# Seven block products instead of eight in the second product of an MLP, on one core

## The chip, the cores and the metric

One core of a Trainium2 chip runs one program for the whole layer. The metric is the time of one execution in microseconds (us) on the device; lower is better. Engines are named as in the profile: PE (TensorE, matrix products), PEld (its weight loads), DVE (VectorE), ACT (ScalarE), POOL (GpSimd), SP (the engine that issues most DMAs). SBUF is the memory that all of them read, PSUM the banks that PE writes.

## The reference

One residual layer over a sequence of 2048 frames of width 1024: a normalisation, forgetting attention with 16 heads, a gated residual, a second normalisation and an MLP with a squared ReLU, all in float32. The change concerns the last product of the last line:

```python
h = rms_norm(x, norm_mlp[i]) * (1 + sc_f) + sh_f
x = x + g_f * (jnp.square(jax.nn.relu(h @ w_mlp_in[i])) @ w_mlp_out[i])
```

Here `h` is 2048 x 1024, `w_mlp_in` 1024 x 4096, `w_mlp_out` 4096 x 1024; `g_f` is one row of 1024 that scales the result.

## The kernel before

The program has stages that follow each other on all engines: projections and attention, the output projection, the MLP's first product, and the MLP's second product, the last stage and the only one that the change touches. A tile framework records the operations in the order in which the code calls them, then orders them on each engine by its own estimate of when each can start, and puts in the waits; so the order on an engine is not quite that of the code.

Float32 products are made from three products of a shorter format. `split` (L749 to L751) writes an operand as two tiles: ACT rounds it to the high part (L750), and DVE subtracts that from the operand to get the low part (L751); both inputs of the subtraction lie in SBUF. `mm3` (L135 to L139) then issues high x high, high x low and low x high into one PSUM bank. A bank holds 128 rows by 512 columns.

The MLP's first product already takes seven block products for each 2x2x2 arrangement of blocks: sums of input blocks are made on POOL (`stage`, L952), split like any operand, multiplied, and the seven results are combined by DVE on the way out of PSUM (`partial`, L987, and `finish`, L980), after which ACT takes the ReLU, POOL the square (L982), and the result `a` goes to DRAM, one tile of 128 features by 512 frames at a time (`a_d`).

The second product, before the change, is plain. The sequence has two halves of 1024 frames (`s`), each of 8 row blocks of 128 frames. The 4096 features are taken in 8 chunks (`ch`) of 4 feature blocks (`CB`). For a chunk, `chunk_ops` loads four blocks of `w2` (128x1024) and eight tiles of `a` (128x512), and splits them; it is a generator that is advanced by one operand between the products of the chunk before. For each row block and each half of the columns, 4 x 3 matmuls sum four feature blocks in one bank (`py`). DVE copies the bank to `ya` in the first chunk (L1110) and adds it in the others (L1118). In the last chunk POOL first multiplies `ya` by the gate and adds the residual `x1`, both 128x1024 (L1101, L1102), and DVE then multiplies the bank by the gate (L1113), adds it (L1114), and the row block is stored.

Of the kernel before, what the change touches and what calls it, by code (L numbers as in the profile page):

```python
# [60 lines left out]
def fox_layer(ctx, tc, x, c, norm_mix, norm_mlp, w_ada, b_ada, w_mlp_in, w_mlp_out,  # L61
              fox_w_in, fox_b_f, fox_q_norm, fox_k_norm, fox_w_out, out):
    nc = tc.nc
    x = x[0]
# [983 lines left out]
    def ring(tag, shape, dt, nm):  # L1050
# [4 lines left out]
    ny = [0]

    def y_bank(nm):
        ny[0] += 1
        if ny[0] % 3 < 2:
            return psS.tile([P, TJ], F32, tag="S", name=nm)  # L1060
        return psT.tile([P, TJ], F32, tag="T", name=nm)

    def chunk_ops(s, ch, into):
        fbs = range(ch * CB, (ch + 1) * CB)
        for t in range(2):
            for fb in fbs:
                if t == 0:
                    wr = ring("wr", [P, D], F32, f"w2r{s}_{fb}")
                    nc.sync.dma_start(wr, w2[fb * P:(fb + 1) * P, :])
                    w = ring("w", [P, 2, D], F32R, f"w2_{s}_{fb}")  # L1070
                    split(w, wr)
                    into["w"].append(w)
                    yield
                ar = ring("ar", [P, TJ], F32, f"ar{s}_{fb}_{t}")
                nc.sync.dma_start(ar, a_d[2 * s + t][fb])
                a = ring("a", [P, 2, TJ], F32R, f"a{s}_{fb}_{t}")
                split(a, ar)
                into["a", t].append(a)
                yield

    steps = [(s, ch) for s in range(NS) for ch in range(NCH)]
    chunks = {st_: {"w": [], ("a", 0): [], ("a", 1): []} for st_ in steps}
    gf = None
    for _ in chunk_ops(*steps[0], chunks[steps[0]]):
        pass
    ya = {}
    for n, (s, ch) in enumerate(steps):
        ops = chunks.pop((s, ch))
        nxt_ = [chunk_ops(*steps[n + 1], chunks[steps[n + 1]])] if n + 1 < len(steps) else []
        if gf is None:  # L1090
            gf = ring("gf", [P, D], F32, "gate_bc1")
            nc.sync.dma_start(gf, gate_d[1:2, :].broadcast_to([P, D]))
        for t in range(2 * RB):
            i = s * 2 * RB + t
            if ch == 0:
                ya[i] = ring("ya", [P, D], F32, f"ya{i}")
            y = ya[i]
            if ch == NCH - 1:
                x1 = ring("x1", [P, D], F32, f"m_x1_{i}")
                nc.sync.dma_start(x1, x1_d[i])  # L1100
                nc.gpsimd.tensor_tensor(y, y, gf, op=ALU.mult)  # L1101
                nc.gpsimd.tensor_tensor(y, y, x1, op=ALU.add)  # L1102
            for hf, cs in enumerate(halves):
                py = y_bank(f"my{n}_{t}_{hf}")
                for b in range(CB):
                    a = ops["a", t // RB][b]
                    mm3(py, (a[:, 0, blk[t % RB]], a[:, 1, blk[t % RB]]),
                        (ops["w"][b][:, 0, cs], ops["w"][b][:, 1, cs]), b == 0, b == CB - 1)
                if ch == 0:
                    nc.vector.tensor_copy(y[:, cs], py)  # L1110
                elif ch == NCH - 1:
                    yg = ring("s", [P, TJ], F32, f"yg{i}_{hf}")
                    nc.vector.tensor_tensor(yg, py, gf[:, cs], op=ALU.mult)  # L1113
                    nc.vector.tensor_tensor(y[:, cs], yg, y[:, cs], op=ALU.add)  # L1114
                    if i >= NT - RB:
                        nc.sync.dma_start(out[i * P:(i + 1) * P, cs], y[:, cs])
                else:
                    nc.vector.tensor_tensor(y[:, cs], py, y[:, cs], op=ALU.add)  # L1118
                if (t, hf) != (RB - 1, 0) and (t, hf) != (RB - 1, 1):
                    run(nxt_)  # L1120
            if ch == NCH - 1 and i < NT - RB:
                nc.gpsimd.dma_start(out[i * P:(i + 1) * P, :], y)
        while nxt_:
            run(nxt_)


# [27 lines left out]
```

## Time and profile before

| | us |
|---|---|
| median of 3 runs | 3043.84 (3041.11 to 3048.27) |
| the profiled execution | 3046.07 |
| its span, first to last instruction | 3044.4 |
| PE busy | 2760.2 (91%) |
| DVE busy | 2078.0 (68%) |
| ACT busy | 1460.2 (48%) |
| POOL busy | 1256.7 (41%) |

The shares are means over stages that differ. The last stage begins when its first operands are loaded, near 2340 us, and ends with the span. A group's row in the profile gives a line of the kernel, engine, operation, tiles written and read, shapes, count, the busy time, the mean of one, and then the idle time of the engine just before them and what ended it.

### The profile page before, as it was taken

To read this page: it belongs to the slowest core of one execution; us is meant where nothing else is said; L and a number is where in the kernel's file an instruction comes from. 1 tells how busy PE (TensorE), PEld (TensorE's weight loads), DVE (VectorE), ACT (ScalarE), POOL (GpSimd) and SP (SyncE) were. 2 spreads that over 40 slices of the span, in tenths; PEclk is the share of its full clock that TensorE was granted. 3 is DMA by queue.
4 is the path that set the end of the run, shared out by engine and by line. 5 is a ranking of instruction groups with operands and counts; after the bars stand their busy time and mean duration, and the time that the engine had idled before them with its cause. 6 is when DMAs were issued, how large, how long until landed. Compare 5 with 4: busy or idle time off the path is not lost. (4 is left out here: it accounts for less than half of the span.)

```text
span 3044.4 us, 45983 instructions
## 1 busy us (share of the span) xinstructions
PE 2760.2 (91%) x16203; PEld 2306.8 (76%) x16203; DVE 2078.0 (68%) x3659; ACT 1460.2 (48%) x2507; POOL 1256.7 (41%) x947
## 2 busy tenths in 40 slices
PE   4788888888889888897899899989998999999999
PEld 4667677777777777786687688878887888888887
DVE  6688987988888887879442765676555544664444
ACT  4466766667667766667352454443333212121210
POOL 3354554646454644544522755575542000500014
PEclk9799989999999999998999899999999999999999
DMA  8479999999999989998963666454444323442322
GB/s 278 129 172 199 217 192 215 208 210 212 215 211 204 210 173 209 180 193 185 197 231 120 186 191 191 152 158 147 139 135 151 128 95 111 138 153 97 111 91 90
DMA packets 867239, 519.22 MB, mean 171 GB/s; under 512 B 590260, under 2 KB 770556, under 8 KB 867008
## 3 DMA queue, kind: packets, MB, share of 16 engines
q1 hardware_dynamic: 862096, 498.98, 66.3%
q0 software_dynamic: 4912, 17.30, 1.6%
q8 instruction: 127, 2.08, 0.3%
q14 instruction: 104, 0.85, 0.1%
HBM read 297.92 MB, written 75.64 MB: 123 GB/s over the span
## 5 line engine op out<-in xcount | busy, mean ns | idle before, releaser
L580 DVE SCALAR_TENSOR_TENSOR ph<-L,ph 128x1024 f16<-128x1024 f32 (+7 forms) x384 | 440.2, 1157 | 81.0 <-ACT ph L568 79.1
L137 PE MATMUL my<-w,a 128*128 128x512 f32 x1024 | 396.6, 391 | 8.2 <-ACT a L750 8.1
L413 POOL TENSOR_TENSOR hl<-hl,hh 128x1024 fp32r<-128x1024 f32 x120 | 299.1, 2494 | 249.3 <-ACT hh L412 218.8
L138 PE MATMUL my<-w,a 128*128 128x512 f32 x1024 | 398.3, 390 | 0.0
L139 PE MATMUL my<-w,a 128*128 128x512 f32 x1024 | 397.4, 389 | 0.0
L568 ACT ACTIVATE ph<-L 128x1024 f16<-128x1024 f32 (+7 forms) x384 | 301.7, 804 | 174.9 <-DMA pT<-ph 150.6
L493 PE MATMUL psq<-w,hh 128*128 128x384 f32 (+1 forms) x960 | 341.2, 356 | 25.1 <-DVE v L502 12.4
L550 DVE CUSTOM_DVE_ANT_0 L<-S,F 128x1024 f32<-128x1024 f32 (+7 forms) x384 | 343.4, 905 | 24.0 <-PE S L546 9.1
L495 PE MATMUL psq<-w,hl 128*128 128x384 f32 (+1 forms) x960 | 353.0, 369 | 2.9 <-POOL hl L413 2.8
L561 ACT ACTIVATE L<-L,st 128x128 f32<-128x128 f32 (+15 forms) x256 | 306.8, 1199 | 92.5 <-DVE st L555 88.5
L494 PE MATMUL psq<-w,hh 128*128 128x384 f32 (+1 forms) x960 | 340.5, 357 | 6.0 <-POOL w L339 6.0
L606 PE MATMUL po<-v,pT 128*128 128x128 f16 x2176 | 276.5, 228 | 69.5 <-DMA pT<-ph 61.1
L543 PE MATMUL S<-kT,qT 128*128 128x512 f32 (+3 forms) x640 | 262.3, 411 | 71.0 <-DVE mx L550 62.0
L1118 DVE TENSOR_TENSOR ya<-my,ya 128x512 f32<-128x512 f32 x192 | 132.0, 689 | 235.8 <-PE my L139 235.7
L606 PEld LDWEIGHTS <-pT 128*128 128x128 f16 x2176 | 204.7, 103 | 100.2 <-DMA pT<-ph 71.9
L1101 POOL TENSOR_TENSOR ya<-ya,gate_bc 128x1024 f32<-128x1024 f32 x16 | 41.1, 2572 | 546.2 <-DVE ya L1118 546.1
L607 PE MATMUL po<-v,pT 128*128 128x64 f16 x2176 | 258.7, 200 | 0.0
L544 PE MATMUL S<-kT,qT 128*128 128x512 f32 (+3 forms) x640 | 241.1, 384 | 0.0
L137 PEld LDWEIGHTS my<-w,a 128*128 128x128 f32 x1024 | 192.8, 188 | 49.1 <-ACT a L750 8.5
L607 PEld LDWEIGHTS <-pT 128*128 128x128 f16 x2176 | 197.7, 101 | 42.6 <-issue 31.7
L750 ACT CAST w<-w2r 128x1024 fp32r<-128x1024 f32 x64 | 67.3, 1051 | 336.3 <-PE my L139 264.0
L138 PEld LDWEIGHTS my<-w,a 128*128 128x128 f32 x1024 | 193.0, 188 | 40.2
(232 smaller groups left out, 6621.4 us busy)
## 6 DMA issues: line engine op xcount, KB each, us to landing
hl<-hT_d SPq DMA_DIRECT2D x120, 512.0 KB
w_Y_A<-in_w_mlp_in_dram SPq DMA_DIRECT2D x128, 256.0 KB
a_d<-c SPq DMA_DIRECT2D x128, 256.0 KB
w2r<-in_w_mlp_out_dram SPq DMA_DIRECT2D x64, 512.0 KB
ar<-a_d SPq DMA_DIRECT2D x128, 256.0 KB
F<-nF_d SPq DMA_DIRECT2D x64, 256.0 KB
wa<-in_w_ada_dram SPq DMA_DIRECT2D x32, 512.0 KB
w_X_A<-in_w_mlp_in_dram SPq DMA_DIRECT2D x64, 256.0 KB
```

The costliest lines, as they stand in the source:

```text
L137: nc.tensor.matmul(ps, lhsT=a[0], rhs=b[0], start=first, stop=False)
L138: nc.tensor.matmul(ps, lhsT=a[0], rhs=b[1], start=False, stop=False)
L139: nc.tensor.matmul(ps, lhsT=a[1], rhs=b[0], start=False, stop=last)
L493: nc.tensor.matmul(ps[:, :n], lhsT=hh, rhs=w[:, 0, :n], start=(kb == 0), stop=False)
L494: nc.tensor.matmul(ps[:, :n], lhsT=hh, rhs=w[:, 1, :n], start=False, stop=False)
L495: nc.tensor.matmul(ps[:, :n], lhsT=hl, rhs=w[:, 0, :n], start=False, stop=(kb == KB - 1))
L550: nc.vector.tensor_tensor_reduce(out=L[:, c0:c1], in0=s2[:, :c1 - c0], in1=Fb[g, h, cch // 2][:, :c1 - c0], scale=1.0, scalar=-3.0e38, op0 ...
L561: nc.scalar.activation(L[:, :W], L[:, :W], AF.Exp, bias=st[:, h:h + 1], scale=1.0, accum_out=st[:, 2 + h:3 + h])
L568: nc.scalar.activation(ph[:, :w], L[:, s0:s0 + w], AF.Copy, scale=PSCALE)
L580: nc.vector.scalar_tensor_tensor(ph[:, w:w + c], L[:, s0:s0 + c], PSCALE, ph[:, :c], op0=ALU.mult, op1=ALU.subtract)
L606: nc.tensor.matmul(po[:, h, :], lhsT=pT[:, bb, :], rhs=v, start=(b == 0), stop=False)
L607: nc.tensor.matmul(po[:, h, 0:HD], lhsT=pT[:, nw + bb, :], rhs=v[:, 0:HD], start=False, stop=(b == nb - 1))
```

## The change

Only the last stage changes. Let the two sequence tiles of a half (512 frames each) be the index t, the two halves of the 4096 features f, and the two halves of the output columns n. Block `A{t}{f}` is a tile of `a`, block `B{f}{n}` a tile of `w2`; feature block p is paired with p + 16. Instead of the eight products A·B, seven products P1 to P7 are made of blocks and of sums of blocks: S1 = A10 + A11, S2 = S1 - A00, S3 = A00 - A10, S4 = A01 - S2, T1 = B01 - B00, T2 = B11 - T1, T3 = B11 - B01, T4 = B10 - T2. The code takes two such pairs of feature blocks at a time (`PC = 2`), so that there are 8 chunks in a half, and of these seven are done in this way. Each of the seven products is summed over the chunks in its own four tiles `E` in SBUF (7 x 4 tiles of 128x512): ACT copies the bank in the first chunk, DVE adds it in the others. In the seventh chunk the tiles are combined to the four results (`merge`, half on POOL, half on DVE). The eighth chunk is done by plain products (`last`, D0 to D3), with gate and residual as before, in tiles of 512 columns.

The sums of blocks run on POOL. Of the 28 splits of a chunk, `ON_POOL` gives the subtraction of 12 to POOL; the other 16 stay on DVE. Sums are called three products ahead of their use, splits two ahead. The split operands have a ring of 16 tiles, four products. The output is stored from SP's queue, where `x1` and all operands are loaded too.

```diff
-    RING = {"wr": 2, "ar": 4, "w": 8, "a": 12, "ya": 10, "gf": 1, "x1": 2, "s": 2}
+    RING = {"rp": 8, "op": 16, "rq": 16, "st": 8, "e": 28, "gf": 1, "x1": 2, "s": 2}
...
-    CB = 4
-    NCH = NFB // CB
+    PC = 2
+    NCH = FP // PC
...
+        def sub(self, dst, op, x, y):
+            for p in self.ps:
+                if dst in ("S1", "S2", "T1", "T2"):
+                    self.r[dst, p] = ring("st", [P, TJ], F32, f"{dst}_{self.s}_{p}")
+                    o = self.r[dst, p]
+                else:
+                    o = self.r[dst, p] = self.r[y if dst in ("S3", "T3") else x, p]
+                nc.gpsimd.tensor_tensor(o, self.r[x, p], self.r[y, p], op=op)
...
+    OPS = {"P1": ("A00", "B00"), "P2": ("A01", "B10"), "P6": ("S2", "T2"), "P7": ("S3", "T3"),
+           "P5": ("S1", "T1"), "P4": ("A11", "T4"), "P3": ("S4", "B11")}
+    ON_POOL = {"P1": 4, "P2": 4, "P5": 2, "P4": 1, "P3": 1}
+
+    def split2(raw, nm, pool):
+        w = ring("op", [P, 2, TJ], F32R, nm)
+        nc.scalar.copy(w[:, 0, :], raw)
+        (nc.gpsimd if pool else nc.vector).tensor_tensor(w[:, 1, :], raw, w[:, 0, :].bitcast(F32), op=ALU.subtract)
+        return w
...
+    def product(chunk, prod):
+        for tb in range(RB):
+            py = y_bank(f"y{prod}_{chunk.s}_{chunk.c}_{tb}")
+            gather(py, chunk.r[prod], tb)
+            if chunk.c == 0:
+                E[prod, tb] = ring("e", [P, TJ], F32, f"e{prod}_{chunk.s}_{tb}")
+                nc.scalar.copy(E[prod, tb], py)
+            else:
+                nc.vector.tensor_tensor(E[prod, tb], E[prod, tb], py, op=ALU.add)
...
+        def add(dst, src):
+            (nc.vector if tb % 2 else nc.gpsimd).tensor_tensor(E[dst, tb], E[dst, tb], E[src, tb], op=ALU.add)
...
+    PORDER = ("P1", "P2", "P6", "P7", "P5", "P4", "P3")
...
+    def base(s, t, n, tb):
+
+        i, y = (2 * s + t) * RB + tb, E[PLACE[t, n], tb]
+        x1 = ring("x1", [P, TJ], F32, f"m_x1_{i}_{n}")
+        nc.sync.dma_start(x1, x1_d[i][:, halves[n]])
+        nc.gpsimd.tensor_tensor(y, y, gf[:, halves[n]], op=ALU.mult)
+        nc.gpsimd.tensor_tensor(y, y, x1, op=ALU.add)
+
+    def last(s, t, n, ops):
+        for tb in range(RB):
+            i, y = (2 * s + t) * RB + tb, E[PLACE[t, n], tb]
+            base(s, t, n, tb)
+            py = y_bank(f"yD{s}_{t}{n}_{tb}")
+            gather(py, ops, tb)
+            yg = ring("s", [P, TJ], F32, f"yg{i}_{n}")
+            nc.vector.tensor_tensor(yg, py, gf[:, halves[n]], op=ALU.mult)
+            nc.vector.tensor_tensor(y, yg, y, op=ALU.add)
+            nc.sync.dma_start(out[i * P:(i + 1) * P, halves[n]], y)
...
+    for n, (chunk, prod) in enumerate(seq):
+        at_sums(n + 3)
+        at_splits(n + 2)
...
+        if prod[0] != "D":
+            product(chunk, prod)
+            if chunk.c == NCH - 2:
+                for tb in range(RB):
+                    merge(prod, chunk.s, tb)
```

Here `gather` is `mm3` over the pairs of a product, and `at_sums` and `at_splits` call the sums and splits of a product and the loads of the next chunk.

**The order on the engines.** DVE in the middle of a half, before: splits of `w2` and `a` between additions to `ya`.

```order
L751 TENSOR_TENSOR w2_0_24_26503<-w2r0_24_26501,w2_0_24_26503 128x1024
L751 TENSOR_TENSOR a0_24_0_26522<-ar0_24_0_26520,a0_24_0_26522 128x512
L1118 TENSOR_TENSOR ya7_25322<-my4_7_1_26473,ya7_25322 128x512
L751 TENSOR_TENSOR w2_0_25_26541<-w2r0_25_26539,w2_0_25_26541 128x1024
L751 TENSOR_TENSOR a0_25_0_26560<-ar0_25_0_26558,a0_25_0_26560 128x512
```

The same engine in the fourth chunk of the first half, with the change (`o` are split operands, `eP3` the tiles `E` of P3, `yP3` banks; the two numbers behind are half and feature block):

```order
L1114 TENSOR_TENSOR oP6S2_0_7_26209<-S2_0_7_26137,oP6S2_0_7_26209 128x512
L1137 TENSOR_TENSOR eP3_0_0_25434<-eP3_0_0_25434,yP3_0_2_0_26159 128x512
L1114 TENSOR_TENSOR oP6T2_0_7_26212<-T2_0_7_26145,oP6T2_0_7_26212 128x512
L1137 TENSOR_TENSOR eP3_0_1_25443<-eP3_0_1_25443,yP3_0_2_1_26167 128x512
L1137 TENSOR_TENSOR eP3_0_2_25452<-eP3_0_2_25452,yP3_0_2_2_26175 128x512
L1137 TENSOR_TENSOR eP3_0_3_25461<-eP3_0_3_25461,yP3_0_2_3_26183 128x512
L1114 TENSOR_TENSOR oP7S3_0_6_26263<-rA10_0_6_25883,oP7S3_0_6_26263 128x512
```

Splits of sums that POOL made (S2, T2, S3) now stand between the evictions of the products before them.

POOL before the change: the last squares of the first product are followed at once by the gate and residual of the first half's end, with nothing between.

```order
L982 TENSOR_TENSOR c10_1_15_24968<-c10_1_15_24968 128x512
L982 TENSOR_TENSOR c01_1_15_24986<-c01_1_15_24986 128x512
L1101 TENSOR_TENSOR ya0_25059<-ya0_25059,gate_bc1_25057 128x1024
L1102 TENSOR_TENSOR ya0_25059<-ya0_25059,m_x1_0_27055 128x1024
L1101 TENSOR_TENSOR ya1_25098<-ya1_25098,gate_bc1_25057 128x1024
```

POOL with the change, from the third chunk (feature blocks 4 and 5) to the fourth (6 and 7); a sum that is written over an input bears the input's name (`rA10` becomes S3):

```order
L1091 TENSOR_TENSOR S1_0_6_26131<-rA10_0_6_25883,rA11_0_6_25887 128x512
L1114 TENSOR_TENSOR oP5S1_0_4_25945<-S1_0_4_25767,oP5S1_0_4_25945 128x512
L1114 TENSOR_TENSOR oP5T1_0_4_25948<-T1_0_4_25775,oP5T1_0_4_25948 128x512
L1091 TENSOR_TENSOR S1_0_7_26133<-rA10_0_7_25885,rA11_0_7_25889 128x512
L1091 TENSOR_TENSOR S2_0_6_26135<-S1_0_6_26131,rA00_0_6_25831 128x512
L1091 TENSOR_TENSOR rA10_0_6_25883<-rA00_0_6_25831,rA10_0_6_25883 128x512
L1114 TENSOR_TENSOR oP4A11_0_4_25991<-rA11_0_4_25523,oP4A11_0_4_25991 128x512
L1091 TENSOR_TENSOR S2_0_7_26137<-S1_0_7_26133,rA00_0_7_25833 128x512
```

The next chunk's sums stand among this chunk's splits; all are 128x512 with two SBUF inputs. At the turn to the second half, POOL with the change:

```order
L1091 TENSOR_TENSOR T2_1_1_28013<-rB11_1_1_27913,T1_1_1_28009 128x512
L1091 TENSOR_TENSOR rB01_1_1_27909<-rB11_1_1_27913,rB01_1_1_27909 128x512
L1168 TENSOR_TENSOR eP3_0_1_25443<-eP3_0_1_25443,m_x1_1_1_27812 128x512
L1168 TENSOR_TENSOR eP3_0_0_25434<-eP3_0_0_25434,m_x1_0_1_27791 128x512
L1114 TENSOR_TENSOR oP2A01_1_0_28015<-rA01_1_0_27499,oP2A01_1_0_28015 128x512
L1114 TENSOR_TENSOR oP2B10_1_0_28018<-rB10_1_0_27503,oP2B10_1_0_28018 128x512
```

The residual additions for the first half's second direct product (L1168) stand between sums and splits of the second half's first chunk.

## Rows read from the trace of the kernel before

**Rows 1.** Windows: busy us (instructions) of PE, PEld, DVE, ACT, POOL; clock, DMA, GB/s.

```profile
2400.00:2590.00 190.00, 190.00 (x840) 157.34 (x839) 88.34 (x122) 37.23 (x52) 0.00 (x0) 1.00 0.29 95
2340.00:3040.60 700.60, 699.06 (x3072) 577.97 (x3072) 367.24 (x480) 137.22 (x191) 88.66 (x44) 1.00 0.36 119
```

**Rows 2.** Chain that ended last, 2300 us to the end: start us, us, what.

```profile
2335.28 3.41 DMA w2r<-in_w_mlp_out_dram
2338.71 1.05 ACT w L750
...
3039.59 0.70 DVE yg L1113
3040.32 0.69 DVE ya L1114
```

**Rows 3.** Groups of the last stage on POOL.

```profile
L1102 POOL TENSOR_TENSOR ya<-ya,m_x 128x1024 f32<-128x1024 f32 x16 | 41.4, 2590 | 1.3
L1101 POOL TENSOR_TENSOR ya<-ya,gate_bc 128x1024 f32<-128x1024 f32 x16 | 41.1, 2572 | 546.2 <-DVE ya L1118 546.1
```

**Rows 4.** Timeline of POOL, 2200 to 2209 us: start us, us, instruction, idle before.

```profile
2201.30 1.29 POOL L952 TENSOR_TENSOR S<-w_Y_A,S 128x512 f32<-128x512 f32 x1
2202.55 1.05 POOL L982 TENSOR_TENSOR c<-c 128x512 f32<-128x512 f32 x1
2205.96 1.29 POOL L952 TENSOR_TENSOR S<-w_Y_A,w_Y_A 128x512 f32<-128x512 f32 x1 [2.36 <-DMA a_d<-c]
2207.20 1.04 POOL L982 TENSOR_TENSOR c<-c 128x512 f32<-128x512 f32 x1
```

**Rows 5.** Timelines of POOL and of DVE, 2026 to 2041 us.

```profile
2032.33 1.71 POOL L952 TENSOR_TENSOR S<-w_Y_A,S 128x512 f32<-128x512 f32 x1
2034.00 1.72 POOL L952 TENSOR_TENSOR S<-w_Y_A,w_Y_A 128x512 f32<-128x512 f32 x1
2035.68 1.49 POOL L982 TENSOR_TENSOR c<-c 128x512 f32<-128x512 f32 x1
2037.13 1.28 POOL L804 TENSOR_TENSOR ht<-hr,ht 128x512 f32<-128x512 f32 x1
...
2029.72 1.52 DVE L751 TENSOR_TENSOR T<-hr,T 128x512 fp32r<-128x512 f32 x1
2031.17 1.74 DVE L751 TENSOR_TENSOR B<-hr,B 128x512 fp32r<-128x512 f32 x1
```

**Rows 6.** Groups of the quiet stretch, 2400 to 2590 us.

```profile
L1118 DVE TENSOR_TENSOR ya<-my,ya 128x512 f32<-128x512 f32 x70 | 48.3, 690 | 90.9 <-PE my L139 90.8
L751 DVE TENSOR_TENSOR a<-ar,a 128x512 fp32r<-128x512 f32 x36 | 23.6, 687 | 3.2 <-ACT a L750 3.2
L750 ACT CAST a<-ar 128x512 fp32r<-128x512 f32 x36 | 21.6, 621 | 61.7 <-PE my L139 60.8
```

**Rows 7.** Windows, 1950 to 2300 us: all; then L751, L980 (DVE), L952, L982 (POOL) alone.

```profile
1950.00:2300.00 350.00, 342.06 (x1493) 282.25 (x1492) 223.49 (x276) 144.25 (x241) 208.25 (x160) 0.99 0.45 142
...
1950.00:2300.00 350.00, 144.90 (x152) 0.99 0.45 142
...
1950.00:2300.00 350.00, 48.11 (x70) 0.99 0.45 142
...
1950.00:2300.00 350.00, 102.10 (x74) 0.99 0.45 142
...
1950.00:2300.00 350.00, 83.49 (x70) 0.99 0.45 142
```

**Rows 8.** Timeline of POOL, 2600 to 2690 us.

```profile
2621.96 2.40 POOL L1102 TENSOR_TENSOR ya<-ya,m_x 128x1024 f32<-128x1024 f32 x1
...
2626.80 2.72 POOL L1102 TENSOR_TENSOR ya<-ya,m_x 128x1024 f32<-128x1024 f32 x1
2630.76 2.77 POOL L1101 TENSOR_TENSOR ya<-ya,gate_bc 128x1024 f32<-128x1024 f32 x1 [1.23 <-DVE ya L1118]
...
2652.93 3.30 POOL L1101 TENSOR_TENSOR ya<-ya,gate_bc 128x1024 f32<-128x1024 f32 x1 [1.23 <-DVE ya L1118]
```

**Rows 9.** Windows, the stretch in which PE starved; columns as in rows 1.

```profile
2020.00:2030.00 10.00, 5.62 (x17) 3.86 (x15) 10.00 (x10) 5.72 (x11) 10.00 (x7) 0.83 0.47 150
```

More of the change, by code (lines that the diff above doesn't have):

```diff
@@ L1058, in y_bank @@
         ny[0] += 1
[L1059 to L1116, printed above, removed]
-                else:
[L1118 to L1124, printed above, removed]
@@ new lines, in fox_layer, with splits @@
+    OPS = {"P1": ("A00", "B00"), "P2": ("A01", "B10"), "P6": ("S2", "T2"), "P7": ("S3", "T3"),
[6 more added lines that the diff above has]
+        return w
+    def splits(chunk, prod):
+        got2 = []
+        for n, (x, p) in enumerate((x, p) for p in chunk.ps for x in OPS[prod]):
+            got2.append(split2(chunk.r[x, p], f"o{prod}{x}_{chunk.s}_{p}", n < ON_POOL.get(prod, 0)))
+        chunk.r[prod] = [(got2[2 * k], got2[2 * k + 1]) for k in range(PC)]
@@ new lines, in gather @@
+    def gather(ps, pairs, tb):
+        for k, (a, b) in enumerate(pairs):
+            mm3(ps, (a[:, 0, blk[tb]], a[:, 1, blk[tb]]), (b[:, 0, :], b[:, 1, :]), k == 0, k == len(pairs) - 1)
+    E = {}
+    def product(chunk, prod):
[7 more added lines that the diff above has]
+                nc.vector.tensor_tensor(E[prod, tb], E[prod, tb], py, op=ALU.add)
@@ new lines, in merge @@
+    def merge(prod, s, tb):
+        def add(dst, src):
+            (nc.vector if tb % 2 else nc.gpsimd).tensor_tensor(E[dst, tb], E[dst, tb], E[src, tb], op=ALU.add)
+        if prod == "P2":
+            add("P2", "P1")
+        elif prod == "P6":
+            add("P6", "P1")
+        elif prod == "P7":
+            add("P7", "P6")
+        elif prod == "P5":
+            add("P6", "P5")
+            add("P5", "P7")
+        elif prod == "P4":
+            add("P4", "P7")
+        elif prod == "P3":
+            add("P3", "P6")
@@ new lines, in last, with group, go @@
+    def last(s, t, n, ops):
[8 more added lines that the diff above has]
+            nc.sync.dma_start(out[i * P:(i + 1) * P, halves[n]], y)
+    def group(chunk, kind, k, nm):
+        names = [f"A{k}{f}" if kind == "A" else f"B{f}{k}" for f in range(2)]
+        for x in names:
+            for p in chunk.ps:
+                chunk.r[nm, x, p] = load2("rq", chunk.s, p, x)
+        def go():
+            return [split2(chunk.r[nm, x, p], f"o{nm}{x}_{chunk.s}_{p}", False) for x in names for p in chunk.ps]
+        return go
@@ new lines, in fox_layer @@
+    seq = []
+    for s in range(NS):
+        for c in range(NCH - 1):
+            seq += [(Chunk(s, c), prod) if prod == "P1" else (None, prod) for prod in PORDER]
+        seq += [(Chunk(s, NCH - 1), f"D{k}") if k == 0 else (None, f"D{k}") for k in range(4)]
+    cur = None
+    for n, (chunk, prod) in enumerate(seq):
+        cur = chunk or cur
+        seq[n] = (cur, prod)
+    nexts = {}
+    plain = [x for n, x in enumerate(y for y, _ in seq) if seq[n][1] == "P1"]
+    for x, y in zip(plain, plain[1:]):
+        nexts[x] = y
@@ new lines, in at_sums, with at_splits @@
+    def at_sums(n):
+        if n >= len(seq):
+            return
+        chunk, prod = seq[n]
+        if prod[0] == "D":
+            return
+        chunk.sums(prod)
+        if prod == "P7" and chunk in nexts:
+            nexts[chunk].load("rp", "A00", "B00")
+        if prod == "P5" and chunk in nexts and nexts[chunk].s == chunk.s:
+            nexts[chunk].load("rq", "A10", "A11", "B01", "B11")
+    def at_splits(n):
+        if n >= len(seq):
+            return
+        chunk, prod = seq[n]
+        if prod[0] != "D":
+            splits(chunk, prod)
+            if prod == "P3" and chunk in nexts:
+                nexts[chunk].load("rp", "A01", "B10")
+        elif prod == "D0":
+            chunk.todo = [group(chunk, "A", 0, "g0"), group(chunk, "B", 0, "g1"), group(chunk, "B", 1, "g2"),
+                          group(chunk, "A", 1, "g3")]
+            chunk.g = [chunk.todo.pop(0)()]
@@ new lines, in fox_layer @@
+    plain[0].load("rp", "A00", "B00", "A01", "B10")
+    plain[0].load("rq", "A10", "A11", "B01", "B11")
+    at_sums(0), at_sums(1), at_sums(2)
+    at_splits(0), at_splits(1)
+    for n, (chunk, prod) in enumerate(seq):
+        at_sums(n + 3)
+        at_splits(n + 2)
+        ahead = seq[n + 1] if n + 1 < len(seq) else (None, "")
+        if ahead[1] == "D0":
+            ahead[0].g.append(ahead[0].todo.pop(0)())
+        if prod[0] != "D":
+            product(chunk, prod)
+            if chunk.c == NCH - 2:
+                for tb in range(RB):
+                    merge(prod, chunk.s, tb)
+        else:
+            k = int(prod[1])
+            if k == 0:
+                chunk.todo.append(group(chunk, "B", 0, "g4"))
+                if chunk.s + 1 < NS:
+                    following = [c for c in plain if c.s == chunk.s + 1][0]
+            if k < 3:
+                chunk.g.append(chunk.todo.pop(0)())
+            if k == 2 and chunk.s + 1 < NS:
+                following.load("rq", "A10", "A11", "B01", "B11")
+            ga, gb = chunk.g[(0, 0, 3, 3)[k]], chunk.g[(1, 2, 2, 4)[k]]
+            last(chunk.s, *((0, 0), (0, 1), (1, 1), (1, 0))[k], list(zip(ga, gb)))
```

34 lines of the change are left out of this document (added).

## The prediction

> **What bounds the kernel now.** Read the windows first: in the last stage, from 2340.0 to 3040.6 us, PE is busy 699.06 of 700.60 us with 3072 matmuls, at a granted clock of 1.00 [rows 1]. That stage is PE and nothing else: in a quiet stretch of it DVE is busy 88 of 190 us and POOL does nothing. Per matmul it is 190.00 / 840 = 0.226 us. The chain of waits gives the stage's two ends: the first operand load is issued at 2335.28 and cast at 2338.71; DVE's last operation begins at 3040.32, and the store takes the rest up to 3044.4 [rows 2].
>
> So fewer matmuls shorten the stage only as long as the work that replaces them goes beside PE. That work goes to POOL and DVE, so the third thing to read is what one of their operations costs alone, and what the two cost each other. The stage before this one, which has the same form of seven products, shows both.
>
> **PE.** 7 chunks x 7 products x 4 row blocks x 2 pairs x 3 matmuls = 1176 in each half, and 4 x 4 x 4 x 3 = 192 for the chunk that stays direct: 2 x 1368 = 2736, 336 fewer. 336 x 0.226 = 76 us is what the change takes off PE, which then needs 2736 x 0.226 = 618 us.
>
> **POOL.** Before, the stage has 16 multiplications of 128x1024 and as many additions on POOL [rows 3]. Now it has 484 operations of 128x512: 224 sums of input blocks, 168 splits, 28 merges, 64 for gate and residual. One alone, with two different SBUF inputs, costs 1.25 us from its start to the next one's (2201.30 to 2202.55, 2205.96 to 2207.20) [rows 4]. 484 x 1.25 = 605 us. That is already 98% of PE's 618.
>
> **DVE beside POOL.** When a DVE operation with two SBUF inputs falls beside a busy POOL, both wait. Where the two alternate, POOL's starts go 2032.33, 2034.00, 2035.68, that is 1.67 and 1.68 us apart in place of 1.25, and DVE's splits take 1.52 and 1.74 us [rows 5] in place of 0.687 alone [rows 6]. So each such DVE operation adds 0.43 us to POOL's queue. DVE operations with one PSUM input are not touched: 48.11 / 70 = 0.687 us in a stretch in which POOL is busy for 60% [rows 7], 0.690 where it does nothing [rows 6]. The change's evictions (E plus a PSUM bank) are of that kind, so I price them at 0.69 us and at nothing for POOL. They have the SBUF operand first, which no row shows; if they contended too, 336 x 0.43 = 144 us would come on top. I give that 0.01 and leave it out.
>
> In the new stage DVE has 324 operations with two SBUF inputs: 264 splits, 28 merges, 32 final adds. 324 x 0.43 = 139 us. The price has two ends. The lower is 0.13, the mean over 1950 to 2300 us, where POOL has gaps that DVE can use: its 160 operations took 208.25 us, where 74 sums at 1.29, 70 squares at 1.04 and 16 others at 1.28 would take 189, so 19 us for 152 DVE splits [rows 4, 5, 7]. With operations twice as wide it is 0.32 to 0.37 (2.72 and 2.77 in place of 2.40) [rows 8]. The upper end is 0.45 (1.74 in place of 1.29). I take 0.43, the row of the same shapes with both queues full, since both will be full: one chunk needs 28 x 1.25 + 16 x 0.43 = 41.9 us of POOL against 168 x 0.226 = 38.0 us of PE, so POOL never gets far enough ahead to have gaps.
>
> The Trainium skill (SBUF — State Buffer, Who interferes with whom) says that a DVE instruction with two SBUF inputs and a GpSimd instruction that reads SBUF exclude each other for the whole instruction, and that a DVE instruction with a single SBUF input does not contend. The second half agrees with [rows 7]. By the first half the price would be DVE's whole 0.69 us and the sum 84 us higher; the alternating rows show 0.43, and they decide.
>
> **What the order adds.** On POOL the sums of the next chunk stand between the splits of this one, as shown above, and P1 and P2 have all four splits there; so a late POOL is felt at once. The ring of split operands holds four products, 4 x 5.4 us of PE, and no queue of finished work builds up in it while POOL is the slowest. At the end of each half POOL has 14 merges and 32 gate and residual operations, 46 x 1.25 = 57.5 us, in the time of PE's direct chunk of 192 x 0.226 = 43 us; in the first half they stand between the sums and splits of the second. DVE's final adds wait for them, PSUM banks wait for DVE, and the residual loads on SP stand behind output stores that wait for DVE. All this is inside POOL's sum as long as POOL does not idle. How much it idles no row shows; with a queue of its own it waited twice for 1.23 us between 2621.96 and 2656, 7% [rows 8]. I take 19 us (2.5% of 744), between 0 and 45.
>
> ACT's 432 casts of 0.62 us [rows 6] and 56 evictions have some 300 us and hide beside POOL. The bytes loaded stay the same, 4.2 MB a chunk, which at 41.9 us is 100 GB/s; the stage moves 95 to 119 now [rows 1].
>
> **Sum.** First POOL split at 2340 (loads issued as now, four of them and ACT's cast ahead of it) [rows 2] + 605 + 139 + 19 + 4 (a last DVE add of 0.7 and the store, 3.4 now [rows 2]) = 3107 us of span. The profiled execution took 3046.07 for its span of 3044.4, 1.7 more, and the median of the runs is 2.2 below it; the two nearly cancel: **3107 us**, 63 us or 2.1% slower. With the price from 0.33 to 0.45 and waits of 0 to 45 us: 3056 to 3140.
>
> PE then idles some 4 us in each chunk. Where it starved in the stage before, with POOL and DVE busy for all of the 10 us, the granted clock was 0.83 in that stretch [rows 9], that is some time at 1.2 GHz. If a gap per chunk costs PE 2 us that way, it needs 40 of POOL's 41.9: nothing yet, but no margin is left.
>
> **Rivals.**
> *POOL gets gaps and DVE uses them* (faster). Place: the splits of P6 and P7, which DVE does. If they fall where POOL waits anyway, the price is 0.13: 324 x 0.13 = 42, and the end is 2340 + 605 + 42 + 19 + 4 = 3010 us. It decides the sign at 0.235 us per operation (3044 - 2340 - 605 - 19 - 4 = 76 us over 324). For it: that mean was measured with the same mix of operations [rows 7]. Against: POOL was busy for 60% there; here its own 28 x 1.25 = 35.0 us a chunk are 92% of PE's 38.0. If POOL did not matter at all, PE would end it: 2341 + 618 + 16 (the third product waits for 21 POOL operations, 26 us, while two products give PE 11) + 5 = 2980 us. Chance 0.14.
>
> *DVE becomes the bound* (slower still). 16 splits at an alternating 1.68 us and 28 evictions at 0.69 are 46.2 us a chunk, 4.3 more than POOL: 14 x 4.3 = 60, so 3167 us. For: DVE was busy 10.00 of 10 us, as POOL was, when PE starved [rows 9]. Against: not each split meets a fresh POOL operation; the mean was 144.90 / 152 = 0.95 us [rows 7]. Chance 0.15.
>
> *The whole DVE instruction counts.* 605 + 324 x 0.69 = 829, so 3191 us. Against it stand POOL's starts 1.67 us apart [rows 5]. It is what the page of the skill named above states. Chance 0.03.
>
> That the change does not do what it says is out: the order has 2736 matmuls of the same shape in the stage where it had 3072.
>
> **Chances and range.** Forecast 0.62; between it and the first rival, at a price near 0.235, no change: 0.05. A measurement of this kernel tells about 0.2%, 6 us, from no change. Faster 0.14, same 0.05, slower 0.62 + 0.15 + 0.03 + 0.01 = 0.81. The range takes the forecast's own, most of the second rival and the way towards the first: 3030 to 3165.
>
> **What would show it.** Right: POOL busy for over 90% of the stage, its sums at a mean of 1.5 us in place of 1.29; DVE's splits at 1.2 to 1.7 us, its evictions at 0.69; PE busy for 85 to 90%, waiting for splits of P1 and P2 that POOL made, and for banks at the halves' ends. Wrong: POOL with gaps while PE is full (first rival); DVE busy throughout while POOL waits for it (second); evictions above 0.69 us.

## The result and the profile after

The changed kernel takes 3115.47 us (median of four runs, 3112.62 to 3118.21). The kernel before took 3042.48 us beside it. The ratio is 1.0238, with a 95% interval of 1.0216 to 1.0259: slower by 73 us. The profiled execution took 3113.41 us for a span of 3111.7. From the last matmul of the MLP's first product to the end of the span, the part that the change touches, it takes 786.1 us (2325.6 to 3111.7) in place of 712.5 before (2331.9 to 3044.4).

The windows are the first view again, for the same stage as in [rows 1]. The columns are the same. The first row is the whole stage up to the end of POOL's work. The next five cut the stretch from 2340 us to the end of the span where a chunk's first matmul stands: the first chunk, then five plain chunks, the turn between the halves (a plain chunk, the direct one, the first of the second half), five plain chunks, and the end.

```profile
2340.00:3108.00 768.00, 661.84 (x2732) 525.23 (x2730) 667.35 (x692) 262.93 (x483) 731.37 (x482) 0.94 0.36 109
...
2340.00:2394.10 54.10, 41.67 (x165) 33.06 (x164) 26.65 (x17) 28.87 (x56) 54.10 (x39) 0.88 0.53 171
2394.10:2612.10 218.00, 199.93 (x841) 159.56 (x840) 202.38 (x217) 80.33 (x148) 213.67 (x145) 0.97 0.33 96
2612.10:2783.90 171.80, 134.23 (x529) 104.95 (x529) 142.41 (x132) 56.52 (x105) 164.07 (x104) 0.88 0.41 129
2783.90:2992.40 208.50, 196.99 (x842) 158.61 (x842) 190.34 (x216) 77.01 (x141) 208.50 (x140) 0.98 0.33 99
2992.40:3111.70 119.30, 89.01 (x361) 69.05 (x359) 105.86 (x114) 20.20 (x37) 91.03 (x58) 0.91 0.29 93
```

POOL, which had nothing to do in most of this stage, is now busy for 731.37 of 768 us, and for 208.50 of 208.50 in the five plain chunks of the second half. PE was busy for all of the stage and is now busy for 86% of it. To see where its time went, take from each stretch what its matmuls need at 0.227 us: 16.6 us are lost in the first chunk, 27.1 and 17.4 in the two runs of five plain chunks, 51.7 at the turn, 37.4 at the end (some 4 of them the last addition and store). Together 150 us, against 76 saved. So two thirds of the loss lie at the start, the turn and the end. The changed kernel's plain chunks take 43.6 us in the first half and 41.7 in the second; PE needs 38.1.

The groups of the stage show what POOL and DVE do, in the form of [rows 3, 6]:

```profile
L1137 DVE TENSOR_TENSOR eP<-eP,yP 128x512 f32<-128x512 f32 x336 | 212.9, 674 | 10.4 <-PE yP L139 10.4
L1114 DVE TENSOR_TENSOR oP6S<-S,oP6S 128x512 fp32r<-128x512 f32 x28 | 57.4, 2051 | 55.7 <-ACT oP6S L1113 55.6
L1168 POOL TENSOR_TENSOR eP<-eP,m_x 128x512 f32<-128x512 f32 x32 | 47.2, 1483 | 17.6 <-DMA m_x<-x_d 17.0 <-DVE oP7S L1114 0.6
L1091 POOL TENSOR_TENSOR rB<-rB,T 128x512 f32<-128x512 f32 x28 | 46.8, 1670 | 0.0
L1091 POOL TENSOR_TENSOR S<-rA,rA 128x512 f32<-128x512 f32 x28 | 45.6, 1643 | 0.7 <-POOL rB L1091 0.7
L1114 DVE TENSOR_TENSOR oP7T<-rB,oP7T 128x512 fp32r<-128x512 f32 x28 | 42.6, 1523 | 0.0
L1114 POOL TENSOR_TENSOR oP1B<-rB,oP1B 128x512 fp32r<-128x512 f32 x28 | 38.8, 1387 | 0.1
```

The evictions, with one operand in PSUM, take 674 ns beside a full POOL, no longer than where POOL does nothing (690 ns in [rows 6]). Splits on DVE, with two SBUF operands, take 1.12 to 2.05 us by group and 1.48 in the mean, in place of 0.687; POOL's sums take 1.40 to 1.67 and 1.57 in the mean, in place of 1.29 (some groups are shown). POOL's sums are idle for 5 us in all: they hardly wait for an operand.

The timelines of POOL and of DVE at the start of a chunk show why (start us, us, instruction, idle before):

```profile
2822.95 1.72 POOL L1114 TENSOR_TENSOR oP1B<-rB,oP1B 128x512 fp32r<-128x512 f32 x1
2824.63 1.74 POOL L1114 TENSOR_TENSOR oP2A<-rA,oP2A 128x512 fp32r<-128x512 f32 x1
2826.33 1.29 POOL L1114 TENSOR_TENSOR oP2B<-rB,oP2B 128x512 fp32r<-128x512 f32 x1
2827.57 1.75 POOL L1114 TENSOR_TENSOR oP2A<-rA,oP2A 128x512 fp32r<-128x512 f32 x1
2829.29 1.73 POOL L1114 TENSOR_TENSOR oP2B<-rB,oP2B 128x512 fp32r<-128x512 f32 x1
```

```profile
2824.06 1.16 DVE L1114 TENSOR_TENSOR oP6T<-T,oP6T 128x512 fp32r<-128x512 f32 x1
2825.14 1.87 DVE L1137 TENSOR_TENSOR eP<-eP,yP 128x512 f32<-128x512 f32 x3
2826.93 1.24 DVE L1114 TENSOR_TENSOR oP7S<-rA,oP7S 128x512 fp32r<-128x512 f32 x1
2828.10 1.78 DVE L1114 TENSOR_TENSOR oP7T<-rB,oP7T 128x512 fp32r<-128x512 f32 x1
```

The POOL operation that starts at 2826.33, while DVE is at three evictions, is followed by the next after 1.24 us (2827.57). Where a DVE split falls beside each, POOL's starts are 1.68 to 1.72 us apart. There the two engines go in lockstep, one split for one POOL operation.

At the turn, the chain of work that ended last runs almost wholly through POOL from 2669 to 2717 us, and mixes the first half's gate with the second half's sums. It begins:

```profile
2668.99 1.65 POOL S L1091
2670.70 3.44 POOL eP L1167 x2
2674.14 1.71 POOL eP L1142
2675.84 1.69 POOL S L1091
2677.53 3.37 POOL eP L1167 x2
```

PE's waits there cost it twice, as its timeline shows:

```profile
2643.04 0.39 PE L139 MATMUL yP<-oP5T,oP5S 128*128 128x512 f32 x1
2646.02 0.47 PE L137 MATMUL yP<-oP4T,oP4A 128*128 128x512 f32 x1 [2.59 <-DVE eP L1137]
...
2647.55 0.63 PE L138 MATMUL yP<-oP4T,oP4A 128*128 128x512 f32 x1
2647.97 0.63 PE L139 MATMUL yP<-oP4T,oP4A 128*128 128x512 f32 x1
```

After a wait of 2.59 us its matmuls soon start 0.42 to 0.43 us apart in place of 0.227, which is the lower of the two clock levels, 1.2 GHz in place of 2.4. Here that lasts to 2649.7. The granted clock of the turn's stretch is 0.88, where this stage had 1.00 before [rows 1].

### The profile page after: what moved, and what is told of

Same layout as the page of the kernel before. It is cut to its first block, busy times and chain, and to the rows that moved or that the text cites. A ratio compares the mean times of both kernels' runs of the same rounds, so it can differ in the third digit from the quotient of the medians.

```text
span 3111.7 us, 46622 instructions
## 1 busy us (share of the span) xinstructions
PE 2719.0 (87%) x15867; PEld 2252.3 (72%) x15867; DVE 2379.0 (76%) x3871; ACT 1589.0 (51%) x2803; POOL 1901.2 (61%) x1387
## 3 DMA queue, kind: packets, MB, share of 16 engines
q8 instruction: 125, 2.05, 0.3%
## 5 line engine op out<-in xcount | busy, mean ns | idle before, releaser
L1137 DVE TENSOR_TENSOR eP<-eP,yP 128x512 f32<-128x512 f32 x336 | 212.9, 674 | 10.4 <-PE yP L139 10.4
L493 PEld LDWEIGHTS psq<-w,hh 128*128 128x128 f32 x960 | 191.1, 199 | 32.3 <-ACT hh L412 14.0
L137 PE MATMUL mP<-T,wP 128*128 128x512 f32 x512 | 203.0, 397 | 4.2 <-ACT T L750 4.1
L138 PE MATMUL mP<-T,wP 128*128 128x512 f32 x512 | 203.7, 398 | 3.3 <-DVE T L751 3.1
L139 PE MATMUL mP<-T,wP 128*128 128x512 f32 x512 | 201.7, 394 | 1.9 <-DVE wP L751 1.9
L982 POOL TENSOR_TENSOR c<-c 128x512 f32<-128x512 f32 x128 | 154.8, 1213 | 73.2 <-ACT c L981 73.0
L494 PEld LDWEIGHTS psq<-w,hh 128*128 128x128 f32 x960 | 189.5, 198 | 13.5 <-POOL w L339 9.9
L543 PEld LDWEIGHTS S<-kT,qT 128*128 128x128 f32 x640 | 126.8, 198 | 99.3 <-DVE mx L550 64.7
```

Of the source, the lines that this page charges most:

```text
L493: nc.tensor.matmul(ps[:, :n], lhsT=hh, rhs=w[:, 0, :n], start=(kb == 0), stop=False)
L494: nc.tensor.matmul(ps[:, :n], lhsT=hh, rhs=w[:, 1, :n], start=False, stop=False)
L543: nc.tensor.matmul(sp, lhsT=q[:, h, qs], rhs=k[:, h, :w], start=True, stop=False)
```

## The experiments

**Control: seven banks in place of eight.** The next run needs a PSUM bank of zeros, so this run takes the bank away without using it. The banks lie in three pools (four, two and two); the sums of products go round the pools, and every fourth goes to the one that is cut from two banks to one.

```
-    psT = ctx.enter_context(tc.tile_pool(name="psT2", bufs=2, space=PSUM))
+    pst = ctx.enter_context(ExitStack())
+    psT = pst.enter_context(tc.tile_pool(name="psT2", bufs=2, space=PSUM))
...
+    pst.close()
+    psT = ctx.enter_context(tc.tile_pool(name="psT3", bufs=1, space=PSUM))
+    psZ = ctx.enter_context(tc.tile_pool(name="psZ", bufs=1, space=PSUM))
+    zero = psZ.tile([P, TJ], F32, tag="Z", name="zero")
+    nc.vector.memset(zero, 0.0)
```

> A control for the next run: one PSUM bank is held by a tile of zeros, so seven banks rotate for the sums of products in place of eight. All theories: no change against the changed kernel, 3115 us, at most +10.

Measured: 3129.39 us, ratio 1.0273 (1.0253 to 1.0294). That is 14 us more than the changed kernel (8 between the profiled spans), a little more than expected. The plain chunks hardly changed: the five of each half take 217.0 and 212.9 us in place of 218.0 and 208.5. The bank is not the only difference, since the framework also orders the operations of POOL and DVE anew for it; what of the 14 us is the bank's was not told apart.

**DVE's splits with one SBUF operand.**

```
         nc.scalar.copy(w[:, 0, :], raw)
-        (nc.gpsimd if pool else nc.vector).tensor_tensor(w[:, 1, :], raw, w[:, 0, :].bitcast(F32), op=ALU.subtract)
+        if pool:
+            nc.gpsimd.tensor_tensor(w[:, 1, :], raw, w[:, 0, :].bitcast(F32), op=ALU.subtract)
+        else:
+            nc.vector.tensor_tensor(w[:, 1, :], zero, raw, op=ALU.subtract)
```

> The splits that DVE makes (264 of them) take a bank of zeros in PSUM and one SBUF operand in place of two SBUF operands; the low part is then not the real one. Theory (POOL's queue, with 0.40 us for each DVE operation of two SBUF inputs): only 60 such operations are left, POOL has 484 x 1.25 + 60 x 0.4 = 629 us of work in place of 734, and the end comes at 2336 + 629 + 36 of gaps + 4 = 3005 us, or at the 2980 to 3005 that PE's own time allows: 2985 to 3015. POOL's operations at 1.3 us, DVE's splits at 0.7. Rival 'the price is not the lock, POOL's operations are long for another reason' (its own operands, DMA traffic): 3115, POOL's splits still at 1.5 to 1.6 us.

Measured: 3016.28 us, ratio 0.9905 (0.9886 to 0.9923), 113 us below its control, with the same number of operations on each engine, and POOL's in nearly the same order in the plain chunks. Windows of three plain chunks, of the control and of this run:

```profile
2829.50:2958.10 128.60, 121.39 (x506) 96.08 (x505) 112.84 (x132) 45.85 (x85) 126.29 (x84) 0.97 0.32 96
```

```profile
2470.50:2584.80 114.30, 114.30 (x506) 94.62 (x505) 82.24 (x132) 45.94 (x85) 105.47 (x85) 1.00 0.36 111
```

A POOL operation takes 126.29 / 84 = 1.50 us beside two-operand splits and 105.47 / 85 = 1.24 beside the others. With 16 of DVE's operations for 28 of POOL's, the difference of 0.26 is 0.46 us for each of them. PE is then full, at 114.30 / 3 = 38.1 us a chunk. The split of T2 on DVE, 1.78 us in the control's stretch, takes 0.68:

```profile
L1123 DVE TENSOR_TENSOR oP6T<-zero,T 128x512 fp32r<-128x512 f32 x6 | 4.1, 680 | 0.0
L1121 POOL TENSOR_TENSOR oP2B<-rB,oP2B 128x512 fp32r<-128x512 f32 x6 | 7.9, 1310 | 0.0
```

The edit also lets the split start without ACT's cast; in the control's stretch no split of DVE waited for a cast, so that does not explain it. This run shows that the second SBUF operand of DVE's splits is what makes POOL's operations long. It frees DVE too, so it does not tell which of the two engines was the bound; the next runs do.

**Half of the evictions off DVE.**

```
-                nc.vector.tensor_tensor(E[prod, tb], E[prod, tb], py, op=ALU.add)
+                if tb % 2:
+                    nc.scalar.copy(E[prod, tb], py)
+                else:
+                    nc.vector.tensor_tensor(E[prod, tb], E[prod, tb], py, op=ALU.add)
```

> The evictions of every second row block go to ACT as plain copies, without the sum (that part of the computation is left out). It takes 168 x 0.68 = 114 us off DVE, 8 a chunk, and nothing off POOL; ACT gets the same and is then busy for some 55%. Theory, POOL's queue is the bound: 3115, at most 20 less. Rival, DVE is the bound: 8 us a chunk less until PE binds, 3020 to 3050.

Measured: 3111.7 us, ratio 1.0229 (1.0204 to 1.0254): the same as the changed kernel. Five plain chunks:

```profile
2783.60:2999.60 216.00, 198.51 (x841) 159.75 (x840) 168.20 (x153) 113.12 (x212) 215.32 (x144) 0.97 0.33 99
```

DVE fell from 91% (190.34 of 208.50) to 78%, POOL stayed at 100%, and the time of the whole stayed (these five chunks take 216.0 us in place of 208.5). DVE was not the bound.

**Fewer splits on POOL: 8, then none, in place of 12 a chunk.**

```
-    ON_POOL = {"P1": 4, "P2": 4, "P5": 2, "P4": 1, "P3": 1}
+    ON_POOL = {"P1": 4, "P2": 4}
```

> Four of POOL's twelve splits of a chunk (those of P5, P4 and P3) go to DVE: POOL 24 x 1.25 + 20 x 0.40 = 38.0 us a chunk in place of 41.9, DVE 20 x 1.44 + 28 x 0.68 = 47.8 in place of 42.1. Theory, POOL alone is the bound: 14 x 3.4 us less, about 3070. Rival, DVE is the bound as much as POOL (87% busy): 14 x (47.8 - 42.5) = 74 more, about 3190. Both bind: near 3115, plus or minus 20.

Measured: 3104.71 us, ratio 1.019 (1.0169 to 1.0212), 11 us below the changed kernel: the third of the expected cases. The plain chunks gain nothing (the five of each half take 215.7 and 212.8 us); the turn and the end do, with 163.5 and 112.0 us in place of 171.8 and 119.3.

```
-    ON_POOL = {"P1": 4, "P2": 4, "P5": 2, "P4": 1, "P3": 1}
+    ON_POOL = {}
```

> All 28 splits of a chunk go to DVE, none to POOL: POOL 16 x 1.25 + 28 x 0.40 = 31 us a chunk, DVE 28 x 0.68 + 28 x 1.1 to 1.4 = 50 to 58. After the run with eight splits on POOL (42.0 us a chunk, DVE busy 98% of the time) DVE is expected to be the bound: 14 x 8 to 14 x 16 us more, 3210 to 3330. If POOL were the bound throughout, it would be faster: 3040.

Measured: 3108.95 us, ratio 1.0219 (1.0188 to 1.0249). This expectation missed by 100 us. Windows of three plain chunks with 8 splits on POOL, and then of four with none:

```profile
2488.40:2614.60 126.20, 118.39 (x506) 94.96 (x505) 126.20 (x146) 46.38 (x85) 109.20 (x72) 0.99 0.33 101
```

```profile
2434.80:2612.70 177.90, 163.13 (x674) 129.46 (x673) 177.90 (x225) 61.19 (x113) 105.71 (x65) 0.96 0.31 95
...
2434.80:2612.70 177.90, 115.25 (x113) 0.96 0.31 95
```

In both DVE is busy for all of the stretch and POOL has gaps. A chunk takes 42.1 and 44.5 us. So DVE takes over as the bound as soon as POOL is relieved, and neither of these two shares makes the plain chunks shorter. That the whole is not slower with none comes from the other parts: the ten plain chunks take 13 us more than the changed kernel's (439.6 against 426.5), the turn and the end 15 less (161.1 and 115.3 us). What I had too high is the price of a split where POOL has gaps: the last row (DVE's splits alone) gives 115.25 / 113 = 1.02 us each. The groups of that stretch say why:

```profile
L1114 DVE TENSOR_TENSOR oP1A<-rA,oP1A 128x512 fp32r<-128x512 f32 x8 | 5.4, 679 | 0.0
L1114 DVE TENSOR_TENSOR oP6S<-S,oP6S 128x512 fp32r<-128x512 f32 x9 | 13.3, 1475 | 0.0
L1091 POOL TENSOR_TENSOR rA<-rA,S 128x512 f32<-128x512 f32 x8 | 14.3, 1786 | 55.3 <-DVE oP2A L1114 55.3
```

POOL waits 55.3 us in these four chunks for the split of A01, whose tile S4 is written over. The splits of P1 that DVE does take 0.679 us each, as alone; those that meet POOL's sums take up to 1.5.

**No sums of the weights.**

```
...
-                self.sub("T1", ALU.subtract, "B01", "B00")
-                self.sub("T2", ALU.subtract, "B11", "T1")
+                self.same("T1", "B01")
+                self.same("T2", "B11")
...
-                self.sub("T3", ALU.subtract, "B11", "B01")
+                self.same("T3", "B11")
...
-                self.sub("T4", ALU.subtract, "B10", "T2")
+                self.same("T4", "B10")
```

> The sums T1 to T4 of the weights' blocks are left out and the blocks themselves used in their place: 8 fewer POOL operations in each of 14 chunks, DVE and PE as they are. Theory (POOL's queue is the bound in the plain chunks): POOL needs 20 x 1.25 + 16 x 0.40 = 31.4 us a chunk, PE's 38.1 binds, 12 x 4.5 us less: about 3060; if the two ends of the halves, where POOL is late too, gain from it as well, down to 3030. Rival, DVE (splits of 1.44 us and evictions, 42 us a chunk) binds as much: at least 3100.

Measured: 3047.08 us, ratio 1.0011 (0.9992 to 1.003), 68 us below the changed kernel and between the theory's two figures. Three plain chunks, the turn, and the end:

```profile
2462.80:2577.00 114.20, 114.20 (x506) 94.56 (x505) 105.04 (x136) 46.14 (x85) 86.03 (x59) 1.00 0.35 111
```

```profile
2577.00:2732.10 155.10, 127.76 (x529) 102.05 (x528) 131.01 (x128) 54.92 (x102) 133.64 (x84) 0.93 0.44 143
2928.20:3038.20 110.00, 86.36 (x361) 69.10 (x359) 95.53 (x109) 19.54 (x36) 78.96 (x50) 0.92 0.30 101
```

With 20 POOL operations in place of 28 a plain chunk takes PE's 38.1 us, at a clock of 1.00. The turn still takes 155.1 us where PE needs 120, and the end 110.0 where it needs 82 and 4.

**No gate and residual on POOL.**

```
-        x1 = ring("x1", [P, TJ], F32, f"m_x1_{i}_{n}")
-        nc.sync.dma_start(x1, x1_d[i][:, halves[n]])
-        nc.gpsimd.tensor_tensor(y, y, gf[:, halves[n]], op=ALU.mult)
-        nc.gpsimd.tensor_tensor(y, y, x1, op=ALU.add)
+        return
```

> The gate's product with E and the addition of the residual are left out on POOL (64 operations, all at the two ends of the halves, with their loads); the plain chunks are as they are. Theory (POOL's queue, at the ends too): 64 x 1.25 = 80 us off POOL's queue, 3035, and the pieces of the ends beyond PE's time (45 and 33 us) nearly gone. Rival, the ends wait for banks, loads or DVE: 3090 or more.

Measured: 3060.52 us, ratio 1.006 (1.0041 to 1.0078): 55 us less, between the two expectations. Plain chunks, turn and end:

```profile
2835.80:2962.50 126.70, 117.99 (x506) 93.49 (x505) 116.31 (x133) 46.00 (x85) 126.70 (x85) 1.00 0.31 96
```

```profile
2615.90:2753.90 138.00, 125.50 (x530) 99.36 (x530) 129.74 (x131) 55.04 (x102) 114.99 (x72) 0.98 0.41 132
2962.50:3057.90 95.40, 83.51 (x361) 66.70 (x359) 86.12 (x114) 20.08 (x37) 41.34 (x26) 0.99 0.22 78
```

The plain chunks stay at POOL's 42.2 us. The turn is 34 us shorter, the end 24; some 18 us of the turn remain beyond PE's time. In it DVE is now the busier of the two (129.74 of 138.00 us, POOL 114.99). POOL's busy time fell by 49 us in the turn and 50 in the end, the time by less: the 80 us of POOL's operations were too much to expect. The run takes the residual's loads away too, for which POOL waited 17.0 us in the changed kernel; it does not tell these from POOL's operations.

**A version without the cause: early sums.** (It ran after the version that follows it, to which its expectation refers.) T1 to T4 depend on the weights alone, and the changed kernel computes them once in each half. Here POOL makes them once, in the stage of the first product, and the last stage loads them (seven blocks in place of four in the second group of a chunk's loads). The rings go with that: 20 tiles in place of 16 for these loads, 6 in place of 8 for the sums.

```
...
+    def prep_w(pp, rest):
+        for p in pp:
...
+            nc.gpsimd.tensor_tensor(t1, b01, b00, op=ALU.subtract)
+            nc.gpsimd.tensor_tensor(t2, b11, t1, op=ALU.subtract)
...
+            nc.gpsimd.tensor_tensor(b01, b11, b01, op=ALU.subtract)
+            nc.gpsimd.tensor_tensor(b10, b10, t2, op=ALU.subtract)
...
+            for k, t in enumerate((t1, t2, b01, b10)):
+                nc.sync.dma_start(t_d[k][p], t)
...
-    RING = {"rp": 8, "op": 16, "rq": 16, "st": 8, "e": 28, "gf": 1, "x1": 2, "s": 2}
+    RING = {"rp": 8, "op": 16, "rq": 20, "st": 6, "e": 28, "gf": 1, "x1": 2, "s": 2}
...
```

> The early T sums alone: gate and residual on POOL as in the changed kernel. Theory: the plain chunks stay at 38.1 us, the ends of the halves keep POOL's 46 operations, and the time stands 20 to 30 us above the version with the shorter ends (3016), so 3036 to 3046, about where the run without T sums stood (3047). Rival, the ends' gain came from the weights' sums too (fewer sums in POOL's queue at the boundary): 3016 to 3025.

Measured: 3034.14 us, ratio 0.9982 (0.9972 to 0.9991), 81 us below the changed kernel. Three plain chunks, turn and end:

```profile
2464.50:2578.70 114.20, 114.20 (x505) 94.58 (x504) 106.72 (x136) 45.85 (x85) 87.86 (x59) 1.00 0.48 157
2578.70:2732.00 153.30, 129.77 (x530) 102.59 (x530) 136.94 (x129) 56.51 (x104) 137.38 (x86) 0.93 0.48 160
2923.80:3033.80 110.00, 86.59 (x361) 69.20 (x359) 95.90 (x110) 19.55 (x36) 78.95 (x50) 0.92 0.31 104
```

It is 18 us above the version below, which has the shorter ends as well, and so a little under the first theory's figure. From the first product's last matmul to the end the two are 28 us apart (705.9 and 677.8), as that theory has it; the last run shows where the other 10 lie. The early sums cost the earlier stage nothing: its matmuls take 657.1 us from first to last in place of the changed kernel's 657.4. In the last stage the DMA carries 157 GB/s in place of 96 and holds nothing up in the plain chunks.

**Early sums and shorter ends.** DVE adds the bank to E and multiplies by the gate; POOL only adds the residual. The residual's loads are called one row block ahead, with three tiles in place of two, and the results on their way out have three tiles of their own.

```
...
-            nc.vector.tensor_tensor(yg, py, gf[:, halves[n]], op=ALU.mult)
-            nc.vector.tensor_tensor(y, yg, y, op=ALU.add)
+            nc.vector.tensor_tensor(yg, y, py, op=ALU.add)
+            nc.vector.tensor_tensor(yg, yg, gf[:, halves[n]], op=ALU.mult)
+            (nc.vector if s == NS - 1 and at == 15 else nc.gpsimd).tensor_tensor(yg, yg, x1, op=ALU.add)
...
```

> A version that should beat both. T1 to T4 depend on the weights alone, so they are made once, on POOL, in the stage of the MLP's first product, where POOL is busy for 50% to 72% of the time, and are loaded in the last stage (56 sums there in place of 112 here). At the ends of the halves DVE adds the PSUM bank to E and multiplies by the gate, and POOL only adds the residual (32 operations in place of 64). Theory: plain chunks at PE's 38.1 us as in the run without T sums (3047 in all), and some 20 to 30 us less at the ends, half of what the run without gate and residual gave; the earlier stage longer by 0 to 15 us: 3020 to 3045. Rival: the seven loads of weight-like blocks a chunk in place of four, or the 56 sums in the earlier stage, where PE starved once beside a full POOL and DVE, take it back: 3050 or more.

Measured: 3016.11 us, ratio 0.9912 (0.9893 to 0.993), 4 us under the theory's range. Its waits (engine, line, what for: us in total, times, longest) show what is left between the halves: DVE stood behind stores, and PE behind DVE.

```profile
DVE yg L1207 <- DMA out_dram<-yg: 18.0, 13, 3.3
PE yP L138 <- DVE yg L1207: 11.5, 3, 6.3
```

**One more tile on the way out.**

```
-    RING = {"rp": 8, "op": 16, "rq": 20, "st": 6, "e": 28, "gf": 1, "x1": 3, "s": 3}
+    RING = {"rp": 8, "op": 16, "rq": 20, "st": 5, "e": 28, "gf": 1, "x1": 3, "s": 4}
```

> The version with early T sums and shorter ends, with four tiles in place of three for the results on their way out, and five in place of six for S1 and S2. In it DVE waited 18.0 us for stores to free such a tile, in 13 places, and PE some 11 us for PSUM banks behind that, between the halves. Theory: 5 to 10 us less, 3006 to 3011. Rival: the fourth tile only moves the wait to POOL's additions or the residual's loads: 3016 plus or minus 3.

Measured: 2999.95 us, ratio 0.9867 (0.9852 to 0.9882), 1.3% faster than the kernel before and 3.7% faster than the changed one. The wait for stores fell to 6.7 us. Plain chunks, turn and end:

```profile
2463.30:2577.60 114.30, 114.30 (x506) 94.62 (x505) 107.88 (x136) 45.97 (x85) 88.25 (x59) 1.00 0.49 155
```

```profile
2577.60:2713.10 135.50, 126.64 (x529) 100.83 (x528) 119.14 (x127) 54.22 (x100) 104.87 (x67) 0.96 0.55 181
2903.60:2996.80 93.20, 82.16 (x361) 67.21 (x359) 87.30 (x110) 19.56 (x36) 50.82 (x33) 0.96 0.36 119
```

The turn is 6.6 us shorter than in the run before (142.1 to 135.5). From the first product's last matmul to the end it is 8.9 us less (677.8 to 668.9), which is the 5 to 10 that the theory has. The rest of the gain between the two profiles, 11 us of 20, lies ahead of the stage that the edit touches. This is the first matmul of the MLP's first product, in the run before and in this one:

```profile
1679.66 0.77 PE L138 MATMUL mP<-B,wP 128*128 128x512 f32 x1 [4.54 <-ACT wP L751]
```

```profile
1670.68 0.79 PE L138 MATMUL mP<-B,wP 128*128 128x512 f32 x1 [4.54 <-ACT wP L751]
```

The run before is 9 us late there, in stages that both kernels have alike. In the profiles of all the kernels here that matmul stands between 1665.3 and 1679.7, so a difference of this size between two spans need not come from the last stage.

## Why the prediction was right

The forecast was 3107 us, and the kernel takes 3115. The mechanism is the one that was forecast, and the terms hold, with three errors (4, 9 and 17 us) that partly cancel; that the total came within 8 us is in part luck.

- **The first POOL split at 2340.** It comes at 2336.20, since the stages ahead ended 6 us sooner in this profile (their last matmul begins at 2325.6, before at 2331.9):

```profile
2336.20 1.26 POOL L1114 TENSOR_TENSOR oP1A<-rA,oP1A 128x512 fp32r<-128x512 f32 x1 [7.69 <-ACT oP1A L1113]
```

- **POOL's own work, 605 us, and DVE beside it, 139 us.** From that split to the end of its last addition at 3107.6 POOL was busy for 735 us; less 605, that is 130 us for 324 operations, 0.40 each, where the sum took 0.43. The rows that gave the 0.43 do not stand beside each other: the DVE splits of 1.52 and 1.74 us lie ahead of POOL's starts at 2032.33 to 2035.68. The price comes from POOL's starts, and it held. In the run of single-operand splits POOL's operations take 1.24 us, which leaves the 1.25 as it was. The price itself is shown by taking it away: 113 us less with the same number of operations.
- **POOL's waits, 19 us.** They are some 36 of the 771 us from its first split to its last addition, 17.0 of them for the residual's loads. This is the term that was mis-sized most. The prediction named these loads on SP, behind stores that wait for DVE, and put nothing beyond the 19 us on them. In the profile they stand in the last 35 us; the ring has two tiles, and each load is issued behind a store.
- **A plain chunk at 41.9 us.** It takes 43.6 in the first half and 41.7 in the second.
- **The evictions at 0.69 us and free of the lock.** They take 674 ns, and the order of operands (SBUF first) makes no difference.
- **PE's margin.** "Nothing yet" was right for the plain chunks: five of them keep POOL at 208.50 of 208.50 us while the clock is 0.98. At the turn and the end PE lost more, at a clock of 0.88 and 0.91. At the turn POOL's queue was still all but full (164.07 of 171.80 us). At the end it was not (91.03 of 119.30): there the residual's loads count as well.
- **First rival (POOL gets gaps).** Out: POOL's gaps are 36 of 771 us, about half of them in the last 35 us.
- **Second rival (DVE is the bound).** Not in this kernel: with 8 us a chunk less on DVE the time stayed. It was nearer than its 46.2 us a chunk told, though: that sum took each split at 1.68 us. With four splits more on DVE, it binds at 42.1 us, no slower than POOL did.
- **Third rival (the whole DVE instruction counts).** Out: 0.40 to 0.46 us against 0.69. The Trainium skill (SBUF — State Buffer, Who interferes with whom) calls the shared port an exclusive lock. The lockstep agrees with that, and so does what takes no part in it, the evictions with one SBUF operand. The price does not agree with a lock over the whole of DVE's instruction: POOL loses 0.40 to 0.46 of the 0.69 us.

What the prediction did not size is the place of PE's loss. It spoke of 4 us in each chunk and named the banks at the halves' ends without a figure; the windows show two thirds of the loss at the start, the turn and the end. As POOL's queue was the bound nearly throughout, its sum gave the time without the place, and so the sum held.

## What to carry to other kernels

When a change trades matmuls for elementwise work, add up the queue of the engine that takes that work, with what its neighbour costs it: here (128x512, float32) a DVE operation with two SBUF operands costs a full POOL 0.40 to 0.46 us, and one with an operand in PSUM costs it nothing. Moving work from POOL to DVE then gains little (11 us for 56 splits), since DVE is bound next; taking work away gains more (68 us without the weights' sums, 81 with half of them gone and half moved to an earlier stage). And look at the ends of a stage by themselves: the steady part can be full while the turn still loses 15 to 50 us (15 in the last version, 52 in the changed kernel).
